# Delta-net on one core: first masked copies of the block inversion on VectorE instead of GpSimd, its tile cleared a step later, and output gates copied out of their banks by ScalarE

## The chip, the core and the metric

The kernel runs on one core of one Trainium2 chip. The metric is the device time of one execution in microseconds (us), as the median of several runs; less is better. Engines are named as in the profile: PE (TensorE matmul), PEld (its weight loads), DVE (VectorE), ACT (ScalarE), POOL (GpSimd) and SP (SyncE, which issues the DMAs).

## What is computed

One inference step of a two-layer decoder over 512 prompt tokens and 8 x 4 sample tokens (544 columns, two halves of 272). Layer 0 has an mLSTM mixer, layer 1 a gated delta-net mixer, and each is followed by a squared-ReLU MLP. The change lies in the delta-net mixer. For each of 16 value heads and each 128-token chunk it solves a unit triangular system and runs a recurrence over chunks; the result is normalised by head and multiplied by an output gate:

```
M = where(strict, einsum('...tk,...sk->...ts', kb, kc) * decay, 0.0)
A = M + eye(L)
sol = triangular_solve(A, rhs, left_side=True, lower=True)
...
o = head_rms(o) * norm_w.reshape(HV_B, DV_B)
o = o.reshape(B, T, VW_B) * silu(z)
return o @ w_out, S, new_conv
```

The kernel inverts A instead of solving: 16 x 16 blocks on DVE, then doubling to 32, 64 and 128 with small matmuls. `silu(z)` is the gate: z times sigmoid(z), here also times the column of norm_w.

## The kernel before

Weights stay in fp32 accuracy by splitting each weight and activation into two parts (`split`: a cast on ACT at L113, a subtraction on DVE at L114), so each projection is three matmuls per 128 x 128 block (`mm3`, L206). A projection of 128 output rows is two halves of 24 matmuls of 272 columns. Each half fills one PSUM bank of the pool `pg` (tile `pg_t`), which has three banks.

The delta-net runs the list `ORDER = "p0 p1 p2 g0 p3 w0 p4 g1 p5 w1 p6 g2 p7 w2 g3 w3"`. A `p` is four projections and their convolutions (`project`, a *unit* of two value heads: keys, queries and two values), a `g` four gate projections (`gate`, four heads), a `w` an output projection of four heads (`out`, operands `gyh` and `gyl`). Each of these steps holds 192 matmuls of L206.

Everything else is fed in between by lanes. After each group of three matmuls `mm3` calls `tick()`, and each lane takes one step of its work (one `yield`) when its period of ticks is over. Lane i takes `prepare` and then `invert` of a unit, lane s `scan` (the recurrence over four chunks), lane d the sample tokens (`decode`, `update`), lane m `gated` (gate times result, and its split, which makes `gyh` and `gyl`). Before each `w` the program calls `finish("m...")`, which runs what is left of the lanes without matmuls of L206 between. The order in which the instructions then stand on each engine is set by a scheduler that takes instructions by this program order, with their waits; engines run their own stream strictly in order.

Names and lines that matter below:

- `prepare` ends with the 16 x 16 inversion on DVE (tb L1151, xb L1153), a DMA of xb to memory (`dx`, L1154), a DMA back in another layout (`xc`, L1156), and then `REST` bare yields.
- `invert` clears X (POOL, L1174), makes DB, two copies of xc masked by block parity (POOL, `tensor_scalar`, L1176), transposes DB into DT on DVE (L1182), and in its next step starts the small matmuls (bank `pm_a`, L1190, then Z on ACT L1192, L1197 and so on); POOL copies DB into X at L1202.
- `scan` has per chunk the matmuls L1280 (St with k and q), L1291 (X), L1298 (state), L1307 (A); then `norm_heads` (squares on ACT L1252, L1253, L1254, product on DVE L1256 into go_on) and the transpose of go_on on PE (L1269).
- `gate` clamps both halves out of their banks (DVE, L1462), runs `sigmoid_chain` on ACT (exp, ln, exp, L523 to L525, 544 columns each) and multiplies by the bank again on DVE (`scalar_tensor_tensor`, L1465). So a bank is held until L1465 has read it.
- `cv` is a ring of four SBUF tiles that the convolutions (`pre`, `acc`) and `gated` (`y`) share.

Of the kernel before, what the change touches and what calls it, by code (L numbers as in the profile page):

```python
# [12 lines left out]
AF = mybir.ActivationFunctionType  # L13
ALU = mybir.AluOpType
# [9 lines left out]
N = TP + NS  # L24
# [18 lines left out]
NX = 2  # L43
# [14 lines left out]
ORDER = "p0 p1 p2 g0 p3 w0 p4 g1 p5 w1 p6 g2 p7 w2 g3 w3"  # L58
PERIODS = {"p0": (6, 5, 6, 4), "w2": (4, 4, 6, 3)}
LAG = 24  # L60
REST = 3

C_GB = 0
C_ANW = 1
C_BNW = C_ANW + 8
# [8 lines left out]
def hybrid_kernel(  # L74
# [26 lines left out]
    V, S, G, T = nc.vector, nc.scalar, nc.gpsimd, nc.tensor  # L101
# [31 lines left out]
    HS = (slice(0, HN), slice(HN, N))  # L133
# [117 lines left out]
    cst = cp.tile([P, C_N], F32, name="cst")  # L251
# [24 lines left out]
    par = cp.tile([P, 3], F32, name="par")  # L276
# [3 lines left out]
    with tc.tile_pool(name="tmpc", bufs=1) as tp:  # L280
        z = tp.tile([P, 512], F32, name="z0")
# [636 lines left out]
    with tc.tile_pool(name="gc", bufs=1, reuse_waits="tile") as gc, ExitStack() as gx:  # L918
# [15 lines left out]
        pss, first = nxt_b  # L934
# [52 lines left out]
        def tl(name, tag=None, bufs=1, n=4, dt=F32):  # L987
            return gp.tile([P, n, P], dt, tag=tag or name, name=name, bufs=bufs)

        def cv(name, n):  # L990
            return gl.tile([P, n], F32, tag="cv", name=name, bufs=NCV)
# [177 lines left out]
        def invert(st):  # L1169


            U, xc = st["U"], st["xc"]
            X = tl("X", n=8, bufs=NX)
            G.memset(X, 0.0)  # L1174
            for q in range(2):
                G.tensor_scalar(DB[:, :, 16 * q:16 * q + 16], xc, par[:, q:q + 1], None, op0=ALU.mult)  # L1176

            def bank(n):
                return mtile()[:, 0:8 * n].rearrange("p (s x) -> p s x", s=8)
# [8 lines left out]
            for s in range(8):  # L1188
                for R in Q:
                    T.matmul(pz[R, s], lhsT=U[R, s, R], rhs=DT[R, s, 0:16], start=True, stop=True,  # L1190
                             tile_position=(R.start, R.start), skip_group_check=True)
            S.activation(Z[:, :, 0:16], pz, AF.Copy, scale=par[:, 2:3])  # L1192
            yield
            px = bank(16)
            for s in range(8):
# [258 lines left out]
        def gate(g):  # L1454

            units[2 * g].update(gates=[], y=([], []))
            for h in range(4):
                pss = proj(wb[12 * g + 8 + h])
                sgm = gb.tile([P, N], F32, tag="yh", name="gsgm", bufs=4)
                units[2 * g]["gates"].append(sgm)  # L1460
                for q in range(2):
                    V.tensor_scalar(sgm[:, HS[q]], pss[q], CLAMP, None, op0=ALU.max)  # L1462
                sigmoid_chain(sgm, None)
                for q in range(2):
                    V.scalar_tensor_tensor(  # L1465
                        sgm[:, HS[q]], pss[q], cst[:, C_BNW + 4 * g + h:C_BNW + 4 * g + h + 1], sgm[:, HS[q]],
                        op0=ALU.mult, op1=ALU.mult)
            done.add(f"g{g}")

        def gated(u):  # L1470
# [208 lines left out]
```

## Time and profile before

| what | value |
|---|---|
| median of 3 runs | 1811.59 us (1808.38 to 1818.83) |
| the profiled execution, its own time | 1804.36 us |
| its span | 1802.5 us |
| instructions | 35688 |
| granted TensorE clock, mean | 0.986 |
| busy PE / PEld / DVE / ACT / POOL | 96% / 92% / 59% / 46% / 4% |
| delta-net stage in the span | about 700 to 1400 us |

The span is what the profiler recorded; the execution's own time has 1.9 us more around it. In the rows further below, a time in brackets is what the engine sat idle before an instruction, and the name behind it the instruction that ended the idle time. A granted clock of 1.00 is 2.4 GHz, and 0.5 is 1.2 GHz; a figure between is the mean of a window in which both occurred.

### The profile page before, as it was taken

The page shows a single profiled execution, that of the slowest core. Times are in us where ns is not written, and L with a number is a line of the kernel's source. Part 1 is how long each engine was busy: PE and PEld are TensorE (multiplying, and loading weights), DVE is VectorE, ACT ScalarE, POOL GpSimd, SP SyncE. Part 2 cuts the span into 40 slices and gives each one's busy share as a digit, 9 for nine tenths or more (in the row PEclk, how much of TensorE's full clock was granted, in tenths as well). Part 3 has the DMA queues.
Part 4 walks back from the last instruction along what each step waited for, and adds up shares of the span by engine and source line. Part 5 has one row for each costly group of instructions (what it writes and reads, how often), then busy time and mean ns, then how long its engine had stood idle before and what let it go on. Part 6 is the DMA issues. An engine that isn't in the chain of part 4 may idle for free.

```text
span 1802.5 us, 35688 instructions
## 1 busy us (share of the span) xinstructions
PE 1723.0 (96%) x14580; PEld 1657.6 (92%) x14580; DVE 1059.6 (59%) x2632; ACT 824.7 (46%) x1874; POOL 66.5 (4%) x121
## 2 busy tenths in 40 slices
PE   7999999999999999999999999989988999999997
PEld 7999998999999999888889889988977999999996
DVE  6564667432244358877966877687668543234436
ACT  5444346331144227865645563656254532134314
POOL 2000000000000000001011010101000000000000
PEclk9999999999999999999999999999998999999999
DMA  4131132222223222223513423241322232223311
GB/s 162 59 104 61 55 116 83 75 90 87 90 84 114 84 87 62 56 61 93 156 50 89 144 65 99 92 125 51 93 94 92 87 95 83 94 83 96 104 59 51
DMA packets 84292, 158.88 MB, mean 88 GB/s; under 512 B 37536, under 2 KB 41504, under 8 KB 83616
## 3 DMA queue, kind: packets, MB, share of 16 engines
q1 hardware_dynamic: 84128, 156.60, 27.8%
q8 instruction: 115, 1.88, 0.4%
q14 instruction: 49, 0.40, 0.1%
HBM read 140.51 MB, written 16.06 MB: 87 GB/s over the span
## 4 chain that ended last, share of the span: by engine, by line
PE 79%; DVE 10%; ACT 5%; DMA 4%; issue 1%; POOL 1%; SPq 0%; ACTq 0%; DVEq 0%; POOLq 0%
PE pg_t L206 39%; PE pm_s L206 12%; PE pm_a L206 12%; PE pm_s L1394 1%; PE pm_s L1445 1%; DVE wl L114 1%; PE pm_s L1280 1%; DMA xc<-dx 1%; DVE lnt L392 1%; DVE lnt L393 1%; DMA dx<-xb 1%; ACT wh L113 1%; PE pm_s L1291 1%; PE pm_a L1116 1%; PE pm_s L1298 1%
## 5 line engine op out<-in xcount | busy, mean ns | idle before, releaser
L114 DVE TENSOR_TENSOR wl<-wraw,wh 128x1024 fp32r<-128x1024 f32 x200 | 245.0, 1225 | 372.5 <-ACT wh L113 371.7
L206 PE MATMUL pg_t<-XH,wh 128*128 128x272 f32 x1480 | 439.5, 297 | 11.9 <-DVE gsgm L1465 6.6
L113 ACT CAST wh<-wraw 128x1024 fp32r<-128x1024 f32 (+1 forms) x201 | 210.1, 1045 | 517.1 <-PE pg_t L206 267.0
L206 PE MATMUL pg_t<-XL,wh 128*128 128x272 f32 x1480 | 434.6, 294 | 0.9 <-issue 0.9
L206 PE MATMUL pg_t<-XH,wl 128*128 128x272 f32 x1480 | 434.2, 294 | 1.1 <-DVE wl L114 1.1
L206 PEld LDWEIGHTS pg_t<-XH,wh 128*128 128x128 f32 x1480 | 280.9, 190 | 17.0 <-DVE gsgm L1465 7.9
L206 PEld LDWEIGHTS pg_t<-XH,wl 128*128 128x128 f32 x1480 | 280.2, 189 | 4.0 <-DVE wl L114 1.8
L206 PEld LDWEIGHTS pg_t<-XL,wh 128*128 128x128 f32 x1480 | 280.9, 190 | 1.9
L206 PE MATMUL pg_t<-h,wh 128*128 128x272 f32 x672 | 129.1, 289 | 0.0
L206 PEld LDWEIGHTS pg_t<-h,wh 128*128 128x128 f32 x672 | 105.6, 188 | 0.3
L206 PE MATMUL pg_t<-h,wl 128*128 128x272 f32 x336 | 96.9, 288 | 0.0
L206 PE MATMUL pm_a<-h,wh 128*128 128x272 f32 x496 | 95.4, 288 | 0.0
L206 PE MATMUL pm_s<-h,wh 128*128 128x272 f32 x496 | 95.0, 288 | 0.0
L206 PE MATMUL pm_s<-XH,wh 128*128 128x272 f32 x288 | 83.3, 289 | 0.8 <-ACT pre L1001 0.8
L206 PE MATMUL pm_s<-XH,wl 128*128 128x272 f32 x288 | 83.1, 288 | 0.0
L206 PE MATMUL pm_a<-XL,wh 128*128 128x272 f32 x280 | 81.9, 292 | 1.0 <-DVE XL L404 0.8
L206 PE MATMUL pm_s<-XL,wh 128*128 128x272 f32 x288 | 82.9, 288 | 0.0
L206 PE MATMUL pm_a<-XH,wh 128*128 128x272 f32 x280 | 82.3, 294 | 0.1
L206 PE MATMUL pm_a<-XH,wl 128*128 128x272 f32 x280 | 81.1, 289 | 0.0
L1010 DVE SCALAR_TENSOR_TENSOR acc<-pre,cst,acc 128x568 f32<-128x568 f32 x96 | 77.3, 805 | 5.1 <-ACT acc L1008 4.6
L206 PEld LDWEIGHTS pm_s<-h,wh 128*128 128x128 f32 x496 | 77.9, 188 | 0.2
L206 PEld LDWEIGHTS pm_a<-h,wh 128*128 128x128 f32 x496 | 78.0, 188 | 0.1
(573 smaller groups left out, 3865.0 us busy)
## 6 DMA issues: line engine op xcount, KB each, us to landing
wraw<-in_w SPq DMA_DIRECT2D x64, 512.0 KB, 3.5
wraw<-in_wb SPq DMA_DIRECT2D x48, 512.0 KB, 3.5
wraw<-in_w2a SPq DMA_DIRECT2D x32, 512.0 KB, 3.4
sst<-in_s SPq DMA_DIRECT2D x64, 256.0 KB, 2.9
wraw<-in_wa SPq DMA_DIRECT2D x24, 512.0 KB, 3.5
wraw<-in_w2b SPq DMA_DIRECT2D x24, 512.0 KB, 3.5
out_ss<-sst SPq DMA_DIRECT2D x32, 256.0 KB, 2.6
wraw<-in_wbo SPq DMA_DIRECT2D x16, 512.0 KB, 3.5
```

The lines of the kernel that those rows point to most:

```text
L113: S.copy(hi, src)
L114: V.tensor_tensor(lo, src, r32(hi), op=ALU.subtract)
L206: T.matmul(ps, lhsT=wt[:, k, :], rhs=xt[k][:, HS[h]], start=first and k == 0 and q == 0, stop=last and k == n - 1 and q == 2,)
L392: V.tensor_tensor(t, x, rs, op=ALU.mult)
L393: V.tensor_tensor(t, t, mu, op=ALU.subtract)
L1010: V.scalar_tensor_tensor(acc, pre[:, q:q + WC], cw[q], acc, op0=ALU.mult, op1=ALU.add)
L1116: T.matmul(pk[:, q * 256:(q + 1) * 256], lhsT=kq[:, 0, c0:c0 + P], rhs=kq[:, :, c0:c0 + P], start=True, stop=True)
L1280: T.matmul(pks[:, w], lhsT=kq[:, w, cc], rhs=St, start=True, stop=True)
L1291: T.matmul(pv[:, j], lhsT=X[:, 4 * (ch // 2) + 2 * j + ch % 2], rhs=rhs[:, j] if ch else vtok[:, j, 0], start=True, stop=True)
L1298: T.matmul(pS, lhsT=ktok[:, ch], rhs=vd, start=True, stop=True)
L1394: T.matmul(pkq[:, r], lhsT=t[:, r], rhs=kqf[:, :, o:o + 4], start=True, stop=True)
L1445: T.matmul(pS, lhsT=KM[:, a], rhs=VM[b], start=(i == 0), stop=(i == 2))
```

## The change

It has four parts. The two masked copies DB of `invert` move from POOL to DVE. X is cleared one step later in `invert`, behind the first small matmuls. `REST` goes from 3 to 5, so `invert` begins two lane steps later in the program. In `gate`, a new tile z in the ring `cv` takes the bank times the norm column by a copy on ACT, and the second reading of the bank (two `scalar_tensor_tensor` of 272 columns on DVE) becomes one `tensor_tensor` of 544 columns in SBUF.

```diff
--- before.py
+++ after.py
@@ -58,7 +58,7 @@
 ORDER = "p0 p1 p2 g0 p3 w0 p4 g1 p5 w1 p6 g2 p7 w2 g3 w3"
 PERIODS = {"p0": (6, 5, 6, 4), "w2": (4, 4, 6, 3)}
 LAG = 24
-REST = 3
+REST = 5
 
 C_GB = 0
 C_ANW = 1
@@ -1170,10 +1170,8 @@
 
 
             U, xc = st["U"], st["xc"]
-            X = tl("X", n=8, bufs=NX)
-            G.memset(X, 0.0)
             for q in range(2):
-                G.tensor_scalar(DB[:, :, 16 * q:16 * q + 16], xc, par[:, q:q + 1], None, op0=ALU.mult)
+                V.tensor_scalar(DB[:, :, 16 * q:16 * q + 16], xc, par[:, q:q + 1], None, op0=ALU.mult)
 
             def bank(n):
                 return mtile()[:, 0:8 * n].rearrange("p (s x) -> p s x", s=8)
@@ -1190,6 +1188,8 @@
                     T.matmul(pz[R, s], lhsT=U[R, s, R], rhs=DT[R, s, 0:16], start=True, stop=True,
                              tile_position=(R.start, R.start), skip_group_check=True)
             S.activation(Z[:, :, 0:16], pz, AF.Copy, scale=par[:, 2:3])
+            X = tl("X", n=8, bufs=NX)
+            G.memset(X, 0.0)
             yield
             px = bank(16)
             for s in range(8):
@@ -1458,13 +1458,12 @@
                 pss = proj(wb[12 * g + 8 + h])
                 sgm = gb.tile([P, N], F32, tag="yh", name="gsgm", bufs=4)
                 units[2 * g]["gates"].append(sgm)
+                z = cv("z", N)
                 for q in range(2):
+                    S.activation(z[:, HS[q]], pss[q], AF.Copy, scale=cst[:, C_BNW + 4 * g + h:C_BNW + 4 * g + h + 1])
                     V.tensor_scalar(sgm[:, HS[q]], pss[q], CLAMP, None, op0=ALU.max)
                 sigmoid_chain(sgm, None)
-                for q in range(2):
-                    V.scalar_tensor_tensor(
-                        sgm[:, HS[q]], pss[q], cst[:, C_BNW + 4 * g + h:C_BNW + 4 * g + h + 1], sgm[:, HS[q]],
-                        op0=ALU.mult, op1=ALU.mult)
+                V.tensor_tensor(sgm, sgm, z, op=ALU.mult)
             done.add(f"g{g}")
 
         def gated(u):
```

The lines of `invert` behind the moved clearing keep their numbers from L1197 on; the copies to DB stand at L1174 in the changed kernel, the transposes at L1180, the first small matmuls at L1188, the clamp at L1464, the product of the gate at L1466.

The scheduler moves much more than the diff shows. Three places, before and after:

**DVE, the last unit (u = 7), from the end of the 16 x 16 inversion (xb) to the first transposition.** Before:

```order
L1153 TENSOR_TENSOR xb<-xb,tb 64x15
L1462 TENSOR_SCALAR gsgm<-pg_t 128x272 x2
L114 TENSOR_TENSOR wl<-wraw,wh 128x1024
L1182 STREAM_TRANSPOSE DT<-DB 128x256
L1465 SCALAR_TENSOR_TENSOR gsgm<-pg_t,cst,gsgm 128x272 x2
```

In the changed kernel:

```order
L1153 TENSOR_TENSOR xb<-xb,tb 64x15
L1464 TENSOR_SCALAR gsgm<-pg_t 128x272
L114 TENSOR_TENSOR wl<-wraw,wh 128x1024
L1464 TENSOR_SCALAR gsgm<-pg_t 128x272
L1174 TENSOR_SCALAR DB<-xc,par 128x8x16 x2
L1180 STREAM_TRANSPOSE DT<-DB 128x256
```

Here the same three instructions stand between; in the first unit there are 18 where 12 stood, in the second 17 for 11, in the third 16 for 21, and in the fourth to eighth 12 for 8, 12 for 6, 7 for 6, 15 for 6 and 3 for 3.

**PE, the start of the last output projection w3 (its operands are `gyh`), where the scan of the last unit ends.** Before:

```order
L206 MATMUL pg_t<-XL_90,wh 128x272
L1269 MATMUL pm_s<-ident,go_on 128x128 x2
L1280 MATMUL pm_s<-St,kq 128x256 x2
L206 MATMUL pg_t<-XH_82,wl 128x272
L1409 MATMUL pm_s<-tok,sx 128x128
L1291 MATMUL pm_s<-rhs,X 128x128 x2
L1298 MATMUL pm_s<-vd,ktok 128x256
L1417 MATMUL pm_s<-sx,UAs 128x128
L1307 MATMUL pm_s<-vn,A 128x128 x2
```

In the changed kernel:

```order
L1307 MATMUL pm_s<-vn,A 128x128 x2
L206 MATMUL pg_t<-XH_82,wh 128x272
L206 MATMUL pg_t<-XL_90,wh 128x272
L206 MATMUL pg_t<-XH_82,wl 128x272
L1400 MATMUL pm_s<-ident,vsxb 128x128
L1400 MATMUL pm_s<-ident,kqs 128x128 x2
L1400 MATMUL pm_s<-ident,kqx 128x128
L1269 MATMUL pm_s<-ident,go_on 128x128 x2
L1280 MATMUL pm_s<-St,kq 128x256 x2
L1409 MATMUL pm_s<-tok,sx 128x128
```

Before, 20 matmuls of L206 stood between the L1307 of this chunk and its L1269, and the transposes L1400 of the sample tokens 18 matmuls ahead of the projection's end; now three matmuls and the four transposes stand there. Behind L1409 the order is the same.

**PE, the start of the first output projection w0, where the scan of unit 1 ends.** Before:

```order
L1269 MATMUL pm_s<-ident,go_on 128x128 x2
L1280 MATMUL pm_s<-St,kq 128x256 x2
L1064 MATMUL pm_t<-onesr,vtokb 128x1 x4
L1291 MATMUL pm_s<-rhs,X 128x128 x2
L1298 MATMUL pm_s<-vd,ktok 128x256
L1307 MATMUL pm_s<-vn,A 128x128 x2
L1051 MATMUL pm_t<-ident,vtokb 128x128 x4
L1269 MATMUL pm_s<-ident,go_on 128x128 x2
```

In the changed kernel:

```order
L1298 MATMUL pm_s<-vd,ktok 128x256
L1307 MATMUL pm_s<-vn,A 128x128 x2
L1051 MATMUL pm_t<-ident,vtokb 128x128 x4
L1269 MATMUL pm_s<-ident,go_on 128x128 x2
L1280 MATMUL pm_s<-St,kq 128x256 x2
L1291 MATMUL pm_s<-rhs,X 128x128 x2
L1338 MATMUL pm_s<-blk,exprow 128x4
L1051 MATMUL pm_t<-ident,vtokb 128x128 x4
L1298 MATMUL pm_s<-vd,ktok 128x256
L1346 MATMUL pm_s<-onesr,kqs 128x1 x2
L1307 MATMUL pm_s<-vn,A 128x128 x2
```

Before, one chunk of the recurrence stood there without a matmul of L206 between; now the end of the chunk before it stands there too, and 18 matmuls of w0 instead of 6 stand ahead of all this.

## Rows read from the trace of the kernel before

**Rows 1.** The page's first part: engines, busy us, share of the span.

```profile
PE 1723.0 (96%) x14580; PEld 1657.6 (92%) x14580; DVE 1059.6 (59%) x2632; ACT 824.7 (46%) x1874; POOL 66.5 (4%) x121
```

**Rows 2.** Who PE waited for, whole span: us in total, times, longest us.

```profile
PE pm_a L1190 <- DVE DT L1182: 7.1, 6, 2.1
PE pg_t L206 <- DVE gsgm L1465: 6.6, 5, 2.5
...
PE pm_a L1190 <- DVE cvo L1003: 2.1, 1, 2.1
```

**Rows 3.** Windows; columns: us, busy of PE, PEld, DVE, ACT, POOL, granted clock, DMA.

```profile
780.00:790.00 10.00, 7.94 (x201) 6.89 (x202) 4.51 (x13) 5.11 (x15) 4.27 (x9) 0.83 0.18 55
...
900.00:910.00 10.00, 6.71 (x150) 6.09 (x151) 6.63 (x20) 4.87 (x17) 2.48 (x4) 0.68 0.15 28
1220.00:1230.00 10.00, 10.00 (x248) 9.03 (x235) 6.42 (x15) 6.23 (x12) 2.99 (x6) 0.83 0.05 14
1330.00:1340.00 10.00, 5.80 (x31) 4.41 (x29) 6.93 (x19) 7.03 (x23) 0.00 (x0) 0.85 0.17 52
...
1350.00:1360.00 10.00, 6.65 (x24) 4.88 (x23) 7.06 (x20) 3.70 (x13) 0.00 (x0) 0.71 0.57 182
```

**Rows 4.** Timeline, gate g2, second head: start us, us, engine, line, operation.

```profile
1192.24 0.43 DVE L1462 TENSOR_SCALAR gsgm<-pg_t 128x272 f32<-128x272 f32 x1
...
1197.55 0.49 DVE L1465 SCALAR_TENSOR_TENSOR gsgm<-pg_t,cst,gsgm 128x272 f32<-128x272 f32 x1
...
1198.10 0.39 PE L206 MATMUL pg_t<-XH,wh 128*128 128x272 f32 x1 [2.54 <-DVE gsgm L1465]
```

**Rows 5.** A group by line on ACT: count, busy us, mean ns, idle before, releaser.

```profile
L999 ACT COPY pre<-pg_t 128x272 f32<-128x272 f32 x30 | 11.4, 381 | 20.0 <-PE pg_t L206 14.9 <-DVE kqx L1022 3.4 <-DVE vsxb L1022 1.5
```

**Rows 6.** Groups by line on DVE, the same columns.

```profile
L114 DVE TENSOR_TENSOR wl<-wraw,wh 128x1024 fp32r<-128x1024 f32 x200 | 245.0, 1225 | 372.5 <-ACT wh L113 371.7
...
L1465 DVE SCALAR_TENSOR_TENSOR gsgm<-pg_t,cst,gsgm 128x272 f32<-128x272 f32 x32 | 15.1, 492 | 1.5 <-ACT gsgm L525 1.2
...
L1477 DVE TENSOR_TENSOR y<-gsgm,oT 128x512 f32<-128x512 f32 x16 | 11.2, 702 | 1.3 <-ACT oT L1271 1.3
...
L1182 DVE STREAM_TRANSPOSE DT<-DB 128x256 f32<-128x256 f32 x16 | 7.1, 443 | 9.6 <-POOL DB L1176 9.5
...
L1405 DVE TENSOR_SCALAR tok<-tok,scolb 128x128 f32<-128x128 f32 x4 | 1.1, 274 | 1.5 <-ACT tok L1402 1.5
```

**Rows 7.** Timeline, POOL and DVE, inversion of u = 1.

```profile
845.65 2.56 POOL L1202 COPY X<-DB 32x256 f32<-32x256 f32 x4 [3.25 <-DVE DB L1199]
...
847.83 0.92 DVE L1477 TENSOR_TENSOR y<-gsgm,oT 128x512 f32<-128x512 f32 x1
```

**Rows 8.** Timeline, block inversion of the first unit (u = 0).

```profile
775.65 0.15 DVE L1153 TENSOR_TENSOR xb<-xb,tb 64x15 f32<-64x15 f32 x1
...
781.48 1.19 POOL L1176 TENSOR_SCALAR DB<-xc,par 128x128 f32<-128x128 f32 x2 [20.18 <-DMA xc<-dx]
782.71 0.45 DVE L1182 STREAM_TRANSPOSE DT<-DB 128x256 f32<-128x256 f32 x1 [1.41 <-POOL DB L1176]
...
783.21 0.73 PE L1190 MATMUL pm_a<-DT,U 32*32 32x16 f32 x64 [2.06 <-DVE DT L1182]
```

**Rows 9.** Timeline, block inversion of the last unit (u = 7).

```profile
1294.97 0.46 SPq L1154 DMA_DIRECT2D dx<-xb  x1
...
1300.29 1.18 POOL L1176 TENSOR_SCALAR DB<-xc,par 128x128 f32<-128x128 f32 x2 [59.90 <-DMA xc<-dx]
```

**Rows 10.** Timeline, PE, inside the last output projection.

```profile
1349.41 0.60 PE L1307 MATMUL pm_s<-vn,A 128*128 128x128 f32 x4
...
1353.14 0.41 PE L1269 MATMUL pm_s<-ident,go_on 128*128 128x128 f32 x2 [2.62 <-DVE go_on L1256]
```

**Rows 11.** Timeline, PE, at the start of the first output projection.

```profile
898.75 0.61 PE L1307 MATMUL pm_s<-vn,A 128*128 128x128 f32 x4
...
902.80 0.41 PE L1269 MATMUL pm_s<-ident,go_on 128*128 128x128 f32 x2 [0.50 <-DVE go_on L1256]
```

## The prediction

> **What bounds the kernel.** I read the page's first part, then PE's waits, then the windows with the granted clock, then single waits in the timeline. PE is busy for 1723.0 of 1802.5 us [rows 1], so all that can be won is in its 79.5 us of idle time and in stretches at the lower clock. The list of its waits [rows 2] names the two that the change touches: L206 waited 6.6 us in five places for the gate's product (L1465), which holds a bank, and L1190 waited 9.2 us (7.1 in six places and 2.1 in one) for the transposed DT or for what stands ahead of it on DVE. The windows [rows 3] show what a long wait also costs: 780 to 790 and 1220 to 1230 us, each with a 2 us wait for DT, ran at a granted clock of 0.83, the stretch at 900 us, where w0 starts, at 0.68, and those at the start of w3 at 0.85 and 0.71. In such a 10 us window (1 - clock) x 10 us is the work lost to the lower level of 1.2 GHz: 1.7 us in each of the first two.
>
> **The gates.** In gate g2 the clamp has read a bank at 1192.67, but the bank comes free only after L1465 of 1197.55, and PE stands for 2.54 us [rows 4]. The change frees it after a copy on ACT and the clamp. A copy of a 272-column bank on ACT takes 381 ns [rows 5]; with a clamp of 430 ns [rows 4] in series behind it the bank is free some 0.8 us after both engines get to it, where the chain before took 5.3 us (1192.67 to 1198.0). The longest of the five waits was 2.5 us, so all five should go: **-6.6 us**. The ends are 0 (ACT comes late to every copy) and -6.6. Added elsewhere: 32 copies x 381 ns = 12.2 us on ACT; on DVE 32 x 492 ns = 15.7 us go (L1465 in [rows 6]) and 16 products of 544 columns come. The nearest row is the 512-column product of `gated` (702 ns, L1477 in [rows 6]), so 0.75 us each, 11.9 us. Both engines have idle time beside PE, so none of this is on the path, and the product's end is needed only by `gated`, steps later.
>
> A product with both operands in SBUF is a form that POOL can get in the way of: beside POOL's four copies (2.56 us, 0.64 each) one took 0.92 us, where 0.70 is the mean [rows 7], [rows 6]. By the row that is 16 x 0.22 = 3.5 us of DVE time at most, off the path, and I put it at nothing. The Trainium skill (SBUF — State Buffer, Who interferes with whom) speaks against the new product: a DVE instruction with two SBUF inputs and a GpSimd instruction that reads SBUF exclude each other, and the later one stands until the first is done. By that rule a product would stand for up to a whole copy, and the sum would be that of rival D and not mine. The row shows a lengthening, but no wait of a whole copy.
>
> **The masked copies.** POOL's pair takes 1.19 us, and DVE waits 1.41 us for it in the first unit, 9.5 us over all 16 transpositions (L1182 in [rows 6]; the first unit in [rows 8]). On DVE 128 columns by `tensor_scalar` take 274 ns (L1405 in [rows 6]), so the pair takes 0.55 us, and a hand-over is saved. That makes 0.6 to 0.7 us per unit once xc has landed, and 16 x 274 ns = 4.4 us more DVE work against 8 x 1.19 = 9.5 us less on POOL [rows 8]. But the copies now wait for the DMA on DVE itself, and all of DVE's stream is held behind them: clamps and splits of weights, which PE needs. From the end of xb (775.80) to POOL's start (781.48) is 5.7 us in the first unit, and 5.3 from dx's issue in the last [rows 8, 9]. DVE must have that much other work in between. From the order and the durations by line I add up what stands there: 5.4, 4.0, 6.3, 1.8, 3.2, 2.0, 2.5 and 2.0 us before, and 7.5, 7.0, 3.6, 5.8, 4.8, 2.4, 5.7 and 2.0 us now (estimates without DVE's own waits, units 0 to 7; in unit 7 two clamps of 0.43 and a split of 1.22 us, L114 in [rows 6]). So `REST` covers the landing in units 0, 1, 3 and 6, almost in 4, and not in 2, 5 and 7. Units 0 and 6 held the two waits of 2.1 us [rows 2], the first at 783 us [rows 8], the other just ahead of 1220. I take that 2.7 of the 9.2 us stay: **-6.5 us**, between 0 and -9.2. With them I take back the clock in the first of the two windows, and half of the second: **-2.5 us**, between 0 and -3.4. Clearing X a step later (POOL, off the path) costs nothing; its cover is that X is first written by POOL itself at L1202.
>
> **What the later inversion pushes out.** The two further lane steps make the scan of a unit later, and where `finish` ends it without projection matmuls to cover, PE waits for it. At w3 the order now has only three matmuls of L206 and four transposes between L1307 and L1269 of a chunk. The same pair stood almost bare once before: from 1349.41 to 1353.14, four matmuls of L206 between, with 2.62 us idle [rows 10]. The transposes of the sample tokens cover a little more: **+2.2 us**, between 0 (that wait overlaps with one that follows) and +2.6. At w0 one more such pair stands in the bare stretch. The pair that stood there took 4.05 us start to start [rows 11] and 3.73 where nothing else held it [rows 10]; the four transposes between cover some 0.6 of that, so 3.1 us stay, and 12 matmuls of w0 have moved ahead and no longer cover the end, which small matmuls of the sample tokens replace in part. I take **+3.5 us**, between +1 and +5.6 (two bare pairs). PE's clock is low in both places; 5.7 us of further idle time there will add to that. The stretch at w3 lost 1.5 + 2.9 us of work by clock in two windows beside 7.5 us of idle time [rows 3]. I take **+1.5 us**, between 0 and +4.
>
> **The sum.** -6.6 - 6.5 - 2.5 + 3.5 + 2.2 + 1.5 = -8.4 us, on an execution of 1804.36 us. That one lies 7 us under the median of the runs shown; against the median of 1811.59 us it gives **1803.2 us**.
>
> **Rivals.**
>
> A. *The full gain.* Both waits go wholly, the two clock dips with them, and the bare stretches at w0 and w3 overlap with waits that are there anyway. For it: a burst on PE with more independent chains (sample tokens beside the scan) hides one behind the other. Against it: engines run in order, and L1269 stands ahead of L1280, which the recurrence needs. -6.6 - 9.2 - 3.4 = -19.2: 1792.4 us.
>
> B. *Slower: the last chunks of the scan are left bare.* The price is the whole stretch at w0 and w3, not a single pair: 900 to 910 us lost 3.3 us idle and 3.2 by clock, and 1330 to 1340 with 1350 to 1360 lost 7.5 and 4.4 [rows 3]. If the two more lane steps repeat the first and add nearly all of the second, +6.5 + 10, and only the gates' 6.6 us come back, since DVE is held by the DMA, the sum is +9.9: 1821.5 us. It decides itself at w3: if PE's idle time in the 10 us around the last projection matmul of g3 (4.2 us in 1330 to 1340 before) more than doubles, this is the case. Against it: the order at w3 shows one pair more, and no whole chunk.
>
> C. *The inversion's wait only moves.* DVE stands at the masked copies for xc as it stood before at the transposition, and the clamps behind it are late. The gates' gain is then eaten by the pairs at w0 and w3: -6.6 + 3.5 + 2.2 + 1.5 = +0.6: 1812.2 us. For it: in units 2, 5 and 7 the work ahead of the copies is less than the landing takes. Against it: four other units now have enough.
>
> D. *POOL's copies hold the gate's product.* The product and the clamps behind it stand for a copy of 0.64 us at the five places of the old waits, 3.2 us: -5.2, 1806.4 us. Against it: POOL runs its copies only in the eight inversions, 4 copies each, and the one row shows 0.22 us. The rule of the Trainium skill named above is this case.
>
> **How the numbers follow.** My forecast has a chance of 0.41, A 0.20, C 0.20, B 0.14, D 0.05. About 0.5%, 9.06 us, is what a measurement of this kernel can tell from no change. The forecast lies at -8.4 with bounds on both sides of that line, so 0.20 of its 0.41 is faster by more; with nearly all of A and a little of D, faster is 0.40. Slower is B and a little of C, 0.17. The rest, 0.43, is the same. The range reaches from just under A to well past C, 1789 to 1819 us, and leaves out B's centre and the far end of A.
>
> **What would show it.** Right, step by step: no wait of L206 for the gate's product or its bank in PE's waits; L1188 waits for DT in sum 2 to 4 us, in units 2 and 7 above all; the granted clock at the first inversion 1.00; at w3 one wait of 2 to 2.6 us more for go_on, and at w0 one of about 3. DVE busy about the same (-3.8 + 4.4 us), ACT 12 us more, POOL 9.5 us less. Wrong: waits of PE for the clamp (L1464) or z of the old size, DVE idle before L1174 of 9 us and more (C), or the stretches at w0 and w3 longer by more than 10 us in all (B).

## The result and the profile after

The changed kernel took 1802.32 us (median of 12 runs, 1786.36 to 1811.37), the kernel before, measured beside it, 1813.50 us (12 runs, 1800.83 to 1821.17). The ratio is 0.9918, 95% interval [0.9892, 0.9944]; a second time, beside the experiments, 0.9885 [0.9853, 0.9918]. The forecast of 1803.2 us lies 0.9 us from the median and the time is inside the range. But that closeness is luck: the kernel before came out 1.9 us above the median that the sum was added to, and the ratio stands for 15 us in 1813.5, interval 10 to 20, where the sum of the prediction was 8.4. The gain came out larger than forecast.

The profiled execution of the changed kernel took 1791.12 us, with a span of 1789.4 us. Its page, first part (columns as in [rows 1]):

```profile
PE 1723.8 (96%) x14580; PEld 1659.9 (93%) x14580; DVE 1055.7 (59%) x2632; ACT 841.9 (47%) x1906; POOL 50.2 (3%) x105
```

PE is idle for 65.6 us (span less busy time) where it was 79.5 [rows 1]. Against [rows 1], DVE has 3.9 us less, ACT 17.2 more (12 were forecast), POOL 16.3 less (9.5 were forecast; beside the masked copies, its copies of L1082 took 5.1 us where they took 9.7, and those of L1202 15.7 for 17.7). Who PE waited for, whole span, the first two rows and the one that answers to [rows 2]:

```profile
PE pm_s L1269 <- DVE go_on L1256: 9.0, 5, 2.6
PE pm_s L1269 <- DVE tb L1151: 5.8, 2, 4.4
...
PE pm_a L1188 <- DVE DT L1180: 0.5, 1, 0.5
```

No wait for the gate's product is left, and of 9.2 us for DT and for what stood ahead of it 0.5 stay. In their place stand waits at L1269, the transposition of go_on at the end of a scan chunk: 3.9 us for go_on before (three places), 9.0 now, and 5.8 behind the 16 x 16 inversion's L1151. A row goes by the instruction that ended last; in the longest wait under tb, 4.37 us at 894.75, go_on itself was made only at 894.60 (DVE's rows below), so that one is a wait for go_on too.

The groups by line of what the change adds (columns as in [rows 5]; for the masked copies and the transposition these answer to the POOL and DVE rows of [rows 6, 8]):

```profile
L1463 ACT ACTIVATE z<-pg_t,cst 128x272 f32<-128x272 f32 x32 | 15.4, 483 | 10.7 <-PE pg_t L206 10.6
L1466 DVE TENSOR_TENSOR gsgm<-gsgm,z 128x544 f32<-128x544 f32 x16 | 11.5, 719 | 7.8 <-ACT gsgm L525 7.6
L1174 DVE TENSOR_SCALAR DB<-xc,par 128x128 f32<-128x128 f32 x16 | 3.8, 281 | 0.5 <-DMA xc<-dx 0.5
L1180 DVE STREAM_TRANSPOSE DT<-DB 128x256 f32<-128x256 f32 x16 | 7.0, 439 | 0.3
```

The copies cost 281 ns each (274 was taken from [rows 6]), and DVE stood for the DMA of xc only once, for 0.5 us. PE's timeline at the start of w0 (its bare stretch in [rows 11]) and in the scan of the last unit:

```profile
888.80 0.68 PE L1307 MATMUL pm_s<-vn,A 128*128 128x128 f32 x4 [0.28 <-DVE xb L1153]
...
894.75 0.66 PE L1269 MATMUL pm_s<-ident,go_on 128*128 128x128 f32 x2 [4.37 <-DVE tb L1151]
...
906.74 0.66 PE L1269 MATMUL pm_s<-ident,go_on 128*128 128x128 f32 x2 [2.45 <-DVE go_on L1256]
...
1319.36 0.66 PE L1269 MATMUL pm_s<-ident,go_on 128*128 128x128 f32 x2 [2.56 <-DVE go_on L1256]
...
1329.51 0.66 PE L1269 MATMUL pm_s<-ident,go_on 128*128 128x128 f32 x2 [1.21 <-DVE go_on L1256]
...
1341.23 0.41 PE L1269 MATMUL pm_s<-ident,go_on 128*128 128x128 f32 x2 [2.37 <-DVE go_on L1256]
```

Two chunk ends stand bare at w0 (4.37 and 2.45 us), and the scan of the last unit has one wait for go_on more (2.56) beside that of [rows 10]; the one of 1.21 us took the place of 0.53 us for y (L1478) in the kernel before. The windows (columns as in [rows 3]) show the first inversion, w0, and the stretches after it:

```profile
780.00:790.00 10.00, 10.00 (x197) 9.56 (x195) 10.00 (x29) 9.53 (x26) 0.34 (x3) 1.00 0.38 83
890.00:900.00 10.00, 4.48 (x18) 3.32 (x17) 9.75 (x40) 4.39 (x12) 0.71 (x1) 0.61 0.34 104
900.00:910.00 10.00, 7.20 (x87) 5.82 (x85) 6.33 (x22) 4.40 (x17) 0.24 (x1) 0.50 0.13 25
910.00:920.00 10.00, 10.00 (x208) 8.90 (x208) 4.70 (x16) 3.34 (x8) 2.76 (x6) 0.86 0.09 28
920.00:930.00 10.00, 10.00 (x80) 9.61 (x78) 4.94 (x12) 4.32 (x13) 0.00 (x0) 1.00 0.37 107
```

780 to 790 us went from 7.94 us busy at 0.83 to 10.00 at 1.00. At w0 PE is idle for 8.3 us in 890 to 910, and the granted clock is 0.61, 0.50 and 0.86 up to 920. What DVE did while PE stood for 4.37 us, from its timeline (the inversion's short L1151 and L1153 stand between):

```profile
891.09 0.40 DVE L1309 TENSOR_TENSOR oi<-oi,pm_s 128x256 f32<-128x256 f32 x1
...
891.80 1.21 DVE L114 TENSOR_TENSOR wl<-wraw,wh 128x1024 fp32r<-128x1024 f32 x1
...
893.34 0.80 DVE L1010 SCALAR_TENSOR_TENSOR acc<-pre,cst,acc 128x568 f32<-128x568 f32 x1
...
894.19 0.41 DVE L1256 TENSOR_TENSOR go_on<-oi,go_ss 128x256 f32<-128x256 f32 x1
```

A split of weights, a convolution and the 16 x 16 inversion of the next unit stand on DVE between oi and the product that PE waits for.

### The profile page after: what moved, and what is told of

The parts are those of the page before. It is cut to its first block, busy times and chain, and to the rows that moved or that the text cites. A ratio compares the mean times of both kernels' runs of the same rounds, so it can differ in the third digit from the quotient of the medians.

```text
span 1789.4 us, 35692 instructions
## 1 busy us (share of the span) xinstructions
PE 1723.8 (96%) x14580; PEld 1659.9 (93%) x14580; DVE 1055.7 (59%) x2632; ACT 841.9 (47%) x1906; POOL 50.2 (3%) x105
## 4 chain that ended last, share of the span: by engine, by line
PE 84%; DVE 8%; ACT 5%; DMA 2%; issue 1%; POOL 0%; SPq 0%; ACTq 0%; DVEq 0%
PE pg_t L206 42%; PE pm_s L206 13%; PE pm_a L206 12%; PE pm_s L1394 1%; PE pm_s L1280 1%; PE pm_s L1445 1%; DVE lnt L392 1%; PE pm_s L1298 1%; PE pm_s L1307 1%; DVE wl L114 1%; DVE lnt L393 1%; PE pm_s L1291 1%; PE pm_t L368 1%; PE pm_a L1116 1%; PE pm_t L1051 1%
## 5 line engine op out<-in xcount | busy, mean ns | idle before, releaser
L206 PE MATMUL pg_t<-XH,wh 128*128 128x272 f32 x1480 | 438.5, 296 | 3.7 <-ACT wh L113 3.6
L206 PE MATMUL pg_t<-XH,wl 128*128 128x272 f32 x1480 | 433.1, 293 | 1.0 <-DVE wl L114 1.0
L206 PE MATMUL pg_t<-XL,wh 128*128 128x272 f32 x1480 | 432.7, 292 | 0.0
L206 PEld LDWEIGHTS pg_t<-XH,wh 128*128 128x128 f32 x1480 | 280.1, 189 | 7.3 <-ACT wh L113 5.0
L206 PEld LDWEIGHTS pg_t<-XH,wl 128*128 128x128 f32 x1480 | 279.3, 189 | 3.1 <-DVE wl L114 1.8
L206 PEld LDWEIGHTS pg_t<-XL,wh 128*128 128x128 f32 x1480 | 280.1, 189 | 1.7
L206 PE MATMUL pg_t<-h,wh 128*128 128x272 f32 x672 | 129.1, 289 | 0.0
L206 PEld LDWEIGHTS pg_t<-h,wh 128*128 128x128 f32 x672 | 105.6, 188 | 0.3
L206 PE MATMUL pg_t<-h,wl 128*128 128x272 f32 x336 | 96.8, 288 | 0.0
L206 PE MATMUL pm_a<-h,wh 128*128 128x272 f32 x496 | 95.3, 288 | 0.0
L206 PE MATMUL pm_s<-h,wh 128*128 128x272 f32 x496 | 94.9, 288 | 0.0
L206 PE MATMUL pm_s<-XH,wh 128*128 128x272 f32 x288 | 83.6, 290 | 0.8 <-ACT pre L1001 0.8
L206 PE MATMUL pm_s<-XH,wl 128*128 128x272 f32 x288 | 83.3, 289 | 0.0
L206 PE MATMUL pm_s<-XL,wh 128*128 128x272 f32 x288 | 83.1, 289 | 0.0
L206 PE MATMUL pm_a<-XL,wh 128*128 128x272 f32 x280 | 81.8, 292 | 0.9 <-DVE XL L404 0.8
L206 PE MATMUL pm_a<-XH,wh 128*128 128x272 f32 x280 | 82.2, 294 | 0.0
L206 PE MATMUL pm_a<-XH,wl 128*128 128x272 f32 x280 | 81.0, 289 | 0.0
L408 DVE SCALAR_TENSOR_TENSOR XR<-XR,pg_t 128x272 f32<-128x272 f32 x118 | 50.8, 432 | 50.5 <-PE pg_t L206 50.1
L206 PEld LDWEIGHTS pm_s<-h,wh 128*128 128x128 f32 x496 | 77.9, 188 | 0.2
```

The costliest lines, as they stand in the source:

```text
L206: T.matmul(ps, lhsT=wt[:, k, :], rhs=xt[k][:, HS[h]], start=first and k == 0 and q == 0, stop=last and k == n - 1 and q == 2,)
L408: V.scalar_tensor_tensor(x, x, ALPHA if first else 1.0, ps, op0=ALU.mult, op1=ALU.add)
```

## The experiments

**How the times are read.** Runs of one kernel differ by up to 1.8%, and most of it goes with the clock: each run lists its span and its mean granted clock, and over all 204 runs of the 12 kernels, taken kernel by kernel, a span grows by 15.5 us for each 0.01 of mean clock that is lost, with about 2 us of scatter around that line. So beside the ratio the table gives each kernel's mean span reduced to a mean clock of 0.975 (standard error 0.2 us for the kernel before, 0.4 to 0.9 for the others). This measure has two limits. It takes out whatever a change does to the clock: ten of the 12 kernels have mean clocks of 0.974 to 0.977, but e6 with 0.971 (standard error 0.0013) and e11 with 0.980 (0.0008) lie outside. And low-clock time in which PE stands idle anyway counts in it, though it costs no work. "Idle" is the span less PE's busy time in the recorded execution. The last three columns are PE's waits for DT, for the gate's product, and for go_on by that name, in us; a wait at L1269 for the same tile that is listed under xb or tb, as the 4 us at w0 in e4, e5, e6, e9 and the changed kernel, is not among them. The changed kernel has 18 runs in two sets.

| kernel | runs | ratio to before | span at 0.975 | idle | DT | product | go_on |
|---|---|---|---|---|---|---|---|
| before (second recording: e8) | 85 | 1 | 1817.3 | 79.5, 77.3 | 7.1, 7.9 | 6.6, 7.0 | 3.9, 3.4 |
| e1 gates alone | 12 | 0.9945 [0.9914, 0.9977] | 1806.5 | 69.1 | 8.5 | 0 | 3.9 |
| e2 copies on DVE alone | 12 | 0.9971 [0.9938, 1.0005] | 1812.1 | 71.1 | 3.8 | 7.8 | 3.4 |
| e4 REST 5 alone | 12 | 0.9959 [0.9928, 0.999] | 1812.0 | 74.1 | 5.8 | 3.7 | 3.8 |
| e3 gates and DVE (REST 3) | 12 | 0.9953 [0.9918, 0.9988] | 1805.9 | 67.2 | 3.3 | 0 | 7.1 |
| e5 DVE and REST 5 | 12 | 0.9932 [0.9901, 0.9962] | 1805.9 | 67.0 | 1.0 | 4.3 | 2.6 |
| e6 gates and REST 5 | 12 | 0.9947 [0.9916, 0.9977] | 1801.5 | 67.7 | 5.8 | 0 | 4.2 |
| changed (all three), e7 | 18 | 0.9918, 0.9885 | 1800.4 | 65.6, 66.6 | 0.5, 0.7 | 0 | 9.0, 9.0 |
| e9 last unit's copies on POOL | 10 | 0.9905 [0.9872, 0.9939] | 1799.5 | 63.5 | 2.6 | 0 | 6.5 |
| e10 REST 6 | 7 | 0.9916 [0.9885, 0.9947] | 1802.5 | 64.3 | 1.3 | 0 | 0.8 |
| e11 REST 4 | 6 | 0.9863 [0.9833, 0.9893] | 1799.9 | 68.1 | 4.7 | 0 | 6.3 |
| e12 w0 one place later | 6 | 0.991 [0.988, 0.994] | 1800.9 | 65.5 | 0 | 0 | 9.6 |

**e1: the gates alone.** On the kernel before, the edit of `gate` only:

```diff
+                z = cv("z", N)
+                    S.activation(z[:, HS[q]], pss[q], AF.Copy, scale=cst[...])
...
-                    V.scalar_tensor_tensor(sgm[:, HS[q]], pss[q], cst[...], sgm[:, HS[q]], ...)
+                V.tensor_tensor(sgm, sgm, z, op=ALU.mult)
```

> The gate part alone on the kernel before (z copied by ACT, product in SBUF; masked copies on POOL, REST 3). Theory 1 (each part gives what its own wait cost): L206's 6.6 us of waits for the gate's product go, L1190's 9.2 us for DT stay within 2 us, the start of w0 stays as before (one bare chunk there: idle 5.3 us and 3.4 us by clock from 890 to 920 us); so -6 to -7 us, ratio about 0.9965. Theory 2 (the gain of the change is in the inversion, the gate's banks are only waited for elsewhere): the same time, ratio 0.999 or more, with waits of PE for the clamp or for ACT's copy in place of the product. Theory 3 (the new order of the instructions decides, parts don't add up): a change of 4 us and more either way that is not in the 6.6 us.

The product's wait is gone. DT's stays, and two others came, a short one for the clamp and, at w0, one of 4.0 us at L1064. PE's waits:

```profile
PE pm_a L1190 <- DVE DT L1182: 7.8, 7, 2.1
...
PE pg_t L206 <- DVE gsgm L1464: 0.6, 1, 0.6
```

The span at equal clock falls by 10.8 us, idle time by 9.3 (to 69.1 from the mean of 79.5 and 77.3). So theory 1 has the wait right, and some 4 us more came, as theory 3 has it. Part of that is idle time that went elsewhere in the new order: the 2.1 us behind cvo [rows 2] are gone too, for one.

**e2: the copies on DVE, X cleared later, alone.**

```diff
-                G.tensor_scalar(DB[:, :, 16 * q:16 * q + 16], xc, par[:, q:q + 1], None, op0=ALU.mult)
+                V.tensor_scalar(DB[:, :, 16 * q:16 * q + 16], xc, par[:, q:q + 1], None, op0=ALU.mult)
...
             S.activation(Z[:, :, 0:16], pz, AF.Copy, scale=par[:, 2:3])
+            X = tl("X", n=8, bufs=NX)
+            G.memset(X, 0.0)
```

> The two masked copies on DVE and X cleared a step later, alone (old gates, REST 3). Theory 1: a hand-over and a slower engine are saved, 0.65 us in each unit where PE waits for DT; of 9.2 us of waits for DT or for what stands ahead of it 5 to 8 us are left, since the landing of xc still comes too late in the units where DVE has 2 to 4 us of other work; L206's 6.6 us for the gate's product stay; -1 to -4 us, ratio 0.998 to 0.9995. Theory 2 (the hand-over is the wait): DT's waits fall under 3 us, and the time by 6 us or more, ratio 0.9965 or less.

Neither theory has the size: 3.8 us of waits for DT are left (5 to 8, or under 3, expected), and 5.2 us are won at equal clock (the ratio alone, with an interval up to 1.0005, shows no change). The hand-over was worth more than I had put it at. DVE itself stood at the copies twice, 3.1 us in all, for xc.

**e3: the changed kernel with REST 3.**

```diff
-REST = 5
+REST = 3
```

> The changed kernel with REST back at 3. Theory 1 (REST 5 buys the landing of xc and pays at w0): waits for DT are 4 to 8 us instead of 0.5, with the clock at the first inversion below 1.00 again, some 8 us given up; the start of w0 is as in the kernel before, 3 us less idle time and about 7 us less by clock, 10 us won. So within 4 us of the changed kernel, ratio against before 0.990 to 0.995. Theory 2 (the hand-over to DVE is the gain, REST only costs): DT's waits stay under 2 us and the time is 8 us and more under the changed kernel, ratio 0.986 to 0.988. At w3 the pair L1307 and L1269 stands with three projection matmuls between here too, so the go_on wait of about 2 us more is to be seen there in this kernel as well, without the two lane steps.

Both theories fail on the time: at equal clock it is 5.5 us above the changed kernel. The masked copies stand for xc on DVE 4.6 us in all (0.5 with REST 5), so the two lane steps do cover the landing:

```profile
L1174 DVE TENSOR_SCALAR DB<-xc,par 128x128 f32<-128x128 f32 x16 | 3.8, 281 | 4.6 <-DMA xc<-dx 4.6
```

At w0 (880 to 930 us) PE is idle for 9.1 us here too, 8.8 in the changed kernel, though at other instructions (L1064 3.1 us, L1051 3.0 us): a bare stretch of that length doesn't need the two lane steps. And the go_on wait in the last scan is there without them:

```profile
1335.73 0.66 PE L1269 MATMUL pm_s<-ident,go_on 128*128 128x128 f32 x2 [2.56 <-DVE go_on L1256]
...
1345.46 0.41 PE L1269 MATMUL pm_s<-ident,go_on 128*128 128x128 f32 x2 [1.21 <-DVE go_on L1256]
...
1357.32 0.41 PE L1269 MATMUL pm_s<-ident,go_on 128*128 128x128 f32 x2 [2.37 <-DVE go_on L1256]
```

**e4: REST 5 alone, in the kernel before.**

```diff
-REST = 3
+REST = 5
```

> REST 5 alone on the kernel before (copies on POOL, old gates). Theory 1: waits for DT fall from 9.2 to 1 to 4 us (-5 to -8, and 2.5 us by clock), the start of w0 gets 10 us longer as in the changed kernel (two chunk ends bare there), the gates' 6.6 us stay, w3 as before; the sum is between -1 and +4 us, ratio 0.9995 to 1.002. Theory 2 (REST only costs): DT's waits stay above 6 us and the time rises by 6 to 10 us, ratio 1.003 to 1.006.

Neither: DT's waits fall only to 5.8 us (1 to 4, or over 6, expected), yet the span falls by 5.3 us at equal clock. DVE still stands 6.2 us for POOL's copies, 9.5 before [rows 6]: with xc in time, POOL's copies and the hand-over alone are left.

```profile
L1182 DVE STREAM_TRANSPOSE DT<-DB 128x256 f32<-128x256 f32 x16 | 7.0, 438 | 6.3 <-POOL DB L1176 6.2
```

So of 9.5 us about two thirds are POOL and its hand-over and one third the landing. The traces split it the same way: of the 9.5 us DVE stood for 2.9 before POOL began and for 6.6 behind that; here it is 0.3 and 5.9. The rest of the gain came with the order: the product's waits fell from 6.6 to 3.7 us with no edit to the gates.

**e5: DVE and REST 5, old gates.** The changed kernel with e1's diff undone:

```diff
-                z = cv("z", N)
...
-                V.tensor_tensor(sgm, sgm, z, op=ALU.mult)
+                    V.scalar_tensor_tensor(sgm[:, HS[q]], pss[q], cst[...], sgm[:, HS[q]], ...)
```

> The inversion part whole (copies on DVE, X cleared later, REST 5) with the old gates. PE's idle time from 700 to 1400 us was 45 us in the kernel before, 39 with the copies on DVE alone and 41 with REST 5 alone. Theory 1 (the two parts remove different waits and add up): 34 to 36 us of idle time, DT's waits under 1 us, time 10 us under the kernel before at the same clock, ratio about 0.994. Theory 2 (both cover the same landing of xc, so the second one adds little): 38 to 41 us of idle time, ratio about 0.9965. In both, L206's waits for the gate's product stay at 4 to 8 us.

Theory 1: 35.8 us of idle time from 700 to 1400 us, DT 1.0 us, 11.4 us won at equal clock, and 5.2 + 5.3 = 10.5 for the two alone. They remove different parts of the same wait.

**e6: the changed kernel with the copies back on POOL,** X cleared ahead of them again.

```diff
-                V.tensor_scalar(DB[...], xc, ...)
+                G.tensor_scalar(DB[...], xc, ...)
```

> The changed kernel with the masked copies back on POOL (and X cleared ahead of them). Theory 1 (POOL's hand-over is a wait of its own): DT's waits come back to 4 to 6 us, as REST 5 alone had 5.8, and the time lies 4 to 6 us above the changed kernel, ratio to before about 0.994. Theory 2 (with the gate's banks free and REST 5, DVE and PE have cover for POOL's 1.2 us too): DT's waits under 2 us and the time of the changed kernel, ratio about 0.991.

DT's waits come back as theory 1 has it:

```profile
PE pm_a L1190 <- DVE DT L1182: 5.8, 6, 1.2
...
PE pm_s L1269 <- DVE go_on L1256: 4.2, 4, 2.5
```

But the span at equal clock is only 1.1 us above the changed kernel (standard error of the difference 0.8), since the go_on waits are 4.2 us here and 9.0 there. On top of the gates' copy, moving the masked copies to DVE takes 5.3 us of waits from PE at DT and gives 4.8 back at go_on. The same stands between e1 and e3 (0.6 us). But the medians differ by 11 us, 1810.5 to 1799.5 on one chip, and the ratios are 0.9947 and 0.9885: this kernel's runs had a mean clock of 0.971 (standard error 0.0013), the changed kernel's there 0.977. What lowers it here was not found, so in time the copies on DVE may still be worth those 11 us; only in waits and at equal clock are they given back.

**e7 and e8: the changed kernel and the kernel before, unaltered, once more.**

> The changed kernel once more, unaltered, for a second recorded execution beside the others on this chip. Theory 1 (the waits are fixed by the order, the low clock after them differs from execution to execution): PE's waits from 640 to 1420 us are the same within 0.5 us each (4.4 us at L1269 for tb, 9.0 us for go_on), but the work lost to the clock from 880 to 930 us, 10.3 us in the first recording, differs by 4 us or more. Theory 2 (the longer idle stretch at w0 sets the clock): 10 us within 2. The ratio to before is 0.990 to 0.993 in both.

> The kernel before once more, unaltered, for a second recorded execution. Theory 1 (the clock differs from execution to execution): the 3.4 us lost to the clock from 880 to 930 us in the first recording, which was among the fastest of this kernel, become another number, up to 10 to 17 us as in the kernels with one part alone, while its waits stay (DT 7.1, gsgm 6.6 us). Theory 2 (the order at w0 sets the clock): 3.4 us again, within 2.

The waits compared repeat to within 0.8 us (tb L1151 5.8 and 6.4 us, go_on 9.0 and 9.0; DT 7.1 and 7.9, product 6.6 and 7.0). The clock doesn't. What is called lost here is (1 - clock) times the length of the windows, as in the prediction, idle time included. In the changed kernel it was 10.3 us at w0 both times (theory 2 of e7, for that place), but 0.0 and 10.2 us from 930 to 1200. In the kernel before it was 3.4 and 8.5 us at w0, and 3.4 and 13.7 us from 770 to 880, where the second recording shows this behind the first inversion:

```profile
780.00:790.00 10.00, 8.52 (x203) 7.20 (x206) 4.16 (x15) 5.32 (x18) 4.21 (x10) 0.64 0.17 55
790.00:800.00 10.00, 10.00 (x93) 9.20 (x86) 1.87 (x6) 4.68 (x9) 0.04 (x1) 0.50 0.02 3
800.00:810.00 10.00, 9.85 (x55) 8.68 (x55) 5.58 (x18) 5.48 (x22) 0.00 (x0) 0.83 0.18 58
```

From 770 to 880 us the idle time is the same (4.2 and 4.1 us), and the loss is four times as large. How long the clock stays low differs between executions of one order. At w0 it still goes with the idle time there: 3.4 to 8.5 us are lost in the three recordings with 3.9 to 5.3 us of idle time (before, e8, e2), and 10 to 20 us in the eleven others, with 5.4 to 9.7.

**e9: the changed kernel, copies of the last unit on POOL.**

```diff
-                V.tensor_scalar(DB[...], xc, ...)
+                (G if st["u"] == 7 else V).tensor_scalar(DB[...], xc, ...)
```

> The changed kernel with the masked copies of the last unit alone back on POOL. PE's order is the changed kernel's up to the last unit; at w3 it is the one without the copies on DVE: the L1307 of a chunk 21 projection matmuls ahead of its L1269 instead of 3. Theory 1 (the copies on DVE, not the two lane steps, bare that pair): the go_on waits at w3 fall by 2 to 5 us (9.0 us in all to 4 to 6), DT's waits rise by at most 1.2 us, and the time at the same clock falls by 1 to 4 us against the changed kernel: ratio to before 0.987 to 0.990. Theory 2 (PE waits there for the recurrence, whatever stands between): go_on's waits move to L1291 or L1298, same time as the changed kernel, ratio 0.989 to 0.992.

In the last scan the extra wait is gone and the other two stand:

```profile
1322.06 0.38 PE L1269 MATMUL pm_s<-ident,go_on 128*128 128x128 f32 x2
...
1331.06 0.66 PE L1269 MATMUL pm_s<-ident,go_on 128*128 128x128 f32 x2 [1.21 <-DVE go_on L1256]
...
1343.50 0.41 PE L1269 MATMUL pm_s<-ident,go_on 128*128 128x128 f32 x2 [2.50 <-DVE go_on L1256]
```

So with the new gates it is the copies on DVE, in the last unit alone, that bare this chunk end. DT's waits rise by 2.1 us (at most 1.2 expected), and the time at equal clock is the changed kernel's (0.9 us less, standard error 0.8, 1 to 4 expected). At w0, where PE's order is the changed kernel's, the clock was low for twice as long:

```profile
900.00:910.00 10.00, 7.20 (x147) 5.76 (x145) 6.31 (x21) 4.44 (x16) 0.00 (x0) 0.50 0.11 21
910.00:920.00 10.00, 10.00 (x126) 8.78 (x119) 3.75 (x11) 2.23 (x7) 2.75 (x6) 0.50 0.04 13
920.00:930.00 10.00, 10.00 (x58) 9.51 (x57) 1.48 (x6) 1.64 (x3) 0.00 (x0) 0.50 0.06 20
930.00:940.00 10.00, 10.00 (x65) 9.49 (x65) 4.95 (x13) 3.43 (x12) 0.00 (x0) 0.86 0.34 102
```

**e10 and e11: the changed kernel with REST 6 and REST 4.**

```diff
-REST = 5
+REST = 6   (e10)
+REST = 4   (e11)
```

> The changed kernel with REST 6. In the order, the scans of units 2, 6 and 7 have more projection matmuls between their steps (at w3 the last transposition stands 7 matmuls before the end, and 20 stand between L1307 and L1269), at w0 two chunk ends stand bare as with REST 5. Theory 1 (DT is covered with 5 already; what is left is the bare stretches at w0 and w3): DT 0 to 1 us, go_on 4 to 6 us instead of 9, w0 as with 5 (idle 8 to 9 us); time at the same clock 2 to 5 us under the changed kernel, ratio to before 0.986 to 0.989. Theory 2 (each lane step more pushes the scan out): idle time at w3 rises by 2 us or more and the ratio is 0.991 or more.

> The changed kernel with REST 4. Theory 1 (REST covers the landing in steps): DT's waits between the 3.3 us of REST 3 and the 0.5 of REST 5, so 1 to 2 us; the pair at w3 as with 3 and 5; two chunk ends bare at w0 as with 5; time at the same clock between the kernels with 3 and 5, ratio to before 0.991 to 0.995. Theory 2 (the order's chance places decide, not the landing): outside of these, by 3 us or more either way.

REST 6 takes go_on's waits down to 0.8 us, but new ones come (L1051 for vtokb 6.5 us, once; L1269 for y 2.8, once), and the span at equal clock is 2.1 us longer: theory 1's gain didn't come. REST 4 leaves 4.7 us for DT (1 to 2 expected) and has the changed kernel's span at equal clock. Its ratio is the lowest of all, but its interval overlaps with the second one of the changed kernel, taken on another chip, and it comes with the highest mean clock (0.980, six runs). That its order is better than the changed kernel's is not shown.

**e12: w0 behind p4.**

```diff
-ORDER = "p0 p1 p2 g0 p3 w0 p4 g1 p5 w1 p6 g2 p7 w2 g3 w3"
+ORDER = "p0 p1 p2 g0 p3 p4 w0 g1 p5 w1 p6 g2 p7 w2 g3 w3"
```

> The changed kernel with the first output projection one place later in the list, behind the projections of unit 4 (p4 w0 instead of w0 p4), so that the end of unit 1's scan stands between projection matmuls: one chunk end (L1307, L1269) is left bare there instead of two, and w0 itself has the scan of unit 2 beside it. Theory 1 (the bare stretch at w0 costs its idle time, 8.8 to 9.0 us in the changed kernel, and the low clock behind it, 10 to 20 us of work in the recordings with this order): idle time from 880 to 930 us falls to 3 to 5 us, what is left of it at the new place included, the low clock there to under 7 us; the time falls by 4 us at the same clock and by 8 to 15 us in all; ratio to before 0.981 to 0.986. Theory 2 (the recurrence of unit 1 is the limit there, wherever the projection stands): the waits move with it to the end of p4, idle time 7 us or more, ratio 0.987 to 0.992 as in the changed kernel.

Idle time from 880 to 930 us falls to 5.4 us, a little above theory 1's 3 to 5, but the time stays the changed kernel's. One bare chunk end is left there, with a wait of 3.13 us for go_on, and the clock fell behind it as it did behind two:

```profile
900.00:910.00 10.00, 5.77 (x108) 4.48 (x112) 7.96 (x28) 5.56 (x21) 0.00 (x0) 0.62 0.28 79
910.00:920.00 10.00, 10.00 (x165) 9.02 (x157) 5.25 (x17) 3.94 (x11) 2.79 (x6) 0.50 0.03 5
```

No version here is shown to beat the changed kernel.

## Why the prediction was right and wrong

**The gates** (-6.6 us). The wait went wholly, as said. The term was too small: alone the edit gives 10.8 us at equal clock. Other waits went with the changed order (that behind cvo); which step of the order moved which wait was not taken apart. Its side terms: the copy on ACT takes 483 ns, not the 381 ns of [rows 5], so 15.4 us rather than 12.2, off the path; the product takes 719 ns, 0.75 us were put.

**The masked copies** (-6.5 us, 2.7 of 9.2 left). 0.5 us is left. The step that failed is the one from DVE's other work to its wait: I had `REST` not covering units 2, 5 and 7. The work ahead of the copies there was as small as I had counted it (3.9, 2.5 and 2.0 us in the changed kernel's trace, 3.6, 2.4 and 2.0 forecast), but I had left out DVE's own waits, and with them it came to the copies 6.0, 8.4 and 6.2 us after xb, when xc had landed. In unit 5 it stood for PE's matmuls of the sample tokens:

```profile
1116.40 0.19 DVE L1396 COPY kqs<-pm_s 128x32 f32<-128x32 f32 x1 [2.38 <-PE pm_s L1394]
1119.56 0.19 DVE L1396 COPY kqs<-pm_s 128x32 f32<-128x32 f32 x1 [2.96 <-PE pm_s L1394]
1119.66 0.47 DVE L1174 TENSOR_SCALAR DB<-xc,par 128x128 f32<-128x128 f32 x2
```

The 0.5 us for xc came in unit 4, "almost" covered in the forecast. The share was wrong as well. I put the gain once xc has landed at 0.6 to 0.7 us per unit and the rest on the landing; e4 has 6.2 of 9.5 us left for POOL once xc is in time, 0.8 per unit, ahead of the 0.56 us that DVE's own pair takes.

**The scan's ends.** w0: +3.5 us forecast, idle time from 880 to 930 us went from 5.3 and 4.2 to 8.8 and 9.0, so +4.2. w3: one wait of 2 to 2.6 us more forecast, 2.56 seen; idle time from 1300 to 1400 went from 14.6 and 13.5 to 15.7 and 15.5, +1.6. Sizes and places were right; the cause was only half right. "The two further lane steps make the scan of a unit later" holds at w0 for REST 5 alone (e4: 8.2 us idle there), but gates and copies on DVE make as long a stretch without it (e3: 9.1). At the last scan it is refuted: e3 has the wait with REST 3, e6 has REST 5 without it, and e9 takes it away by one unit's copies. The order shows where a stretch lies bare, and not which edit put it there.

**The clock** (-2.5 and +1.5 us). This step can't be made as I made it. The first window did go to 1.00, but the second went the other way: from 1200 to 1300 us the clock was 0.98 in both recordings of the kernel before and 0.95 and 0.97 in those of the changed one, which has no wait for DT there. e8 shows that the 1.7 us lost in the first window in [rows 3] was a small draw (the loss from 770 to 880 was 3.4 us in one recording and 13.7 in the other), and the kernel before was read from one of its fastest executions. The price was wrong too: (1 - clock) times a window counts idle time, which the low clock doesn't lengthen. Only at w0 does the sign hold (e7 and e8 above). Mean clocks of before and changed are 0.9753 and 0.9766 (standard error 0.001 for the second): no difference shown.

**The sum.** -8.4 us forecast, 16.9 at equal clock. Of these 12.3 us are PE's idle time (78.4 to 66.1, means of two recordings), where the idle terms summed to -7.4. The further 5 us come from DT (2) and waits of the convolutions and the scan that the new order removed. Of the remaining 4.6 us, 2.0 belong to the measure: of the clock's low time 12.5 and 17.6 us fell into PE's idle time in the recordings of the kernel before, and 19.4 and 18.8 in those of the changed one, where it costs no work but counts in the mean clock. The last 2.6 us I can't place; PE's busy time, less half of what lay at the low clock, differs by more than that between the two recordings of the kernel before (1704.7 and 1701.4 us, 1699.7 and 1700.9 in the changed kernel). By the prediction's own line of 0.5% the kernel is faster, which had a chance of 0.40, and not the same (0.43).

**The rivals.** A, the full gain (-19.2), is closest to the gain (15 by the ratio, 16.9 at equal clock), and its first half holds: both waits go. Its second half doesn't: of the two clock dips one went and one deepened, and neither stretch overlapped with what was there. B: the stretches at w0 and w3 grew by 6 us of idle time together, not by whole chunks, and PE was idle for 2.6 us in the 10 us around the last projection matmul of g3 (1311 to 1321), not for twice 4.2. C: DVE's wait for xc is 0.5 us. D: the product showed 719 ns in the mean and stood for no copy, since none ran beside it; what such a meeting costs is in the last section.

What the prediction had no term for is that the parts don't add at equal clock: alone they give 10.8, 5.2 and 5.3 us, 21.3 in all, together 16.9 (standard error of the difference 1.1). By the ratios alone, whose intervals are 5 us to either side for each part, it couldn't be told. Gates and REST 5 add up (15.8 against 16.1), DVE and REST 5 too, gates and DVE don't (11.4 against 16.0, standard error 1.0): what the copies on DVE win at DT, the scan gives back at go_on.

## What to carry to other kernels

Where a scheduler sets the order, the wait that an edit removes is a fair forecast of that wait, and a poor one of the time: build each part alone, and look for what the whole gives back. Where the clock differs between runs, compare kernels by their spans at equal mean clock beside the ratio, knowing that this leaves out what the change does to the clock; take idle time from the recording, but not the clock. A bank held over a long chain was worth more here than the waits charged to it (10.8 us against 6.6).

## What was not expected of the hardware

A copy of a 128x272 bank on ACT with a scale for each partition took 483 ns (L1463) where a plain copy of the same shape takes 383 (L999 in the changed kernel).

After a few us of idle time PE's clock fell to the lower level of 1.2 GHz and stayed there through fully busy windows, for a time that differed between executions of one kernel: behind the first inversion (780 to 810 us) the windows were at 0.83, 1.00 and 1.00 in one recording of the kernel before and at 0.64, 0.50 and 0.83 in the other. Counting only low-clock time in which PE was busy, it cost 7.0 us at w0 in both recordings of the changed kernel and 17.6 in e9, beside some 9 us of idle time in all three.

A DVE instruction with both operands in SBUF beside a copy of POOL: the one that begins later can stand. In the kernel before, POOL's L1204 took 1.30 us beside a split of weights, where it takes 0.39 in six of eight inversions:

```profile
1059.03 1.29 DVE L114 TENSOR_TENSOR wl<-wraw,wh 128x1024 fp32r<-128x1024 f32 x1 [1.57 <-ACT wh L113]
```

```profile
1059.29 1.30 POOL L1204 COPY ZX<-DT 32x256 f32<-32x256 f32 x1
```

The new product did the same in e3's inversion of the second unit (first row DVE, others POOL):

```profile
846.47 0.77 DVE L1466 TENSOR_TENSOR gsgm<-gsgm,z 128x544 f32<-128x544 f32 x1
```

```profile
844.84 1.82 POOL L1202 COPY X<-DB 32x256 f32<-32x256 f32 x4 [14.79 <-DVE DB L1199]
846.72 0.77 POOL L1203 COPY ZX<-DT 32x256 f32<-32x256 f32 x1
847.53 0.39 POOL L1204 COPY ZX<-DT 32x256 f32<-32x256 f32 x1
```

L1203 took 0.77 us where it takes 0.39 in six of eight inversions of the changed kernel. Both copies end 0.25 to 0.27 us behind the DVE instruction that began before them. The product itself, begun when L1202 had 0.19 us to run, took 0.77 us where e3's mean is 0.718. In [rows 7] POOL's four copies end at 848.21, so the product there began when they had 0.38 us to run, not 2.56, and took 0.22 us more than the mean. The Trainium skill (SBUF — State Buffer, Who interferes with whom) has the later of two such instructions stand until the first is done; these rows agree with it: each time the later one is lengthened by what the first had left to run, less 0.12 to 0.16 us. So the prediction was wrong to read its row against that rule, and right that it costs this kernel nothing: in the changed kernel no gate product met a copy of POOL, only the clearing of X (709 and 715 ns beside it, against 719 in the mean).
